# A decoder layer on one core: raw tiles of the gate block, the branch projections and the down projection laid out anew

## The chip, the cores and the metric

The kernel runs on 1 core of one Trainium2 chip. The metric is device time in microseconds, from start to end of one execution. The core's engines each run their own list of instructions in order: PE (matrix multiply, with its weight loads shown as PEld), DVE (vector), ACT (activation), POOL (GpSimd) and SP, which here issues most of the DMAs. They wait for each other by semaphores.

## What is computed

One layer of a decoder on x of 1024 positions by 1024 channels in float32. What matters for this change:

```python
g_m, g_d, g_c = jnp.split(jax.nn.sigmoid(h @ w_gate[l] + b_gate[l]), N_BRANCH, axis=-1)
merged = g_m * (y_m @ w_proj_m[l]) + g_d * (y_d @ w_proj_d[l]) + g_c * (y_c @ w_proj_c[l])
x = x + merged @ w_out[l]

h2 = rms_norm(x, norm_mlp_g[l])
x = x + jnp.square(jax.nn.relu(h2 @ w_up[l])) @ w_down[l]
```

h is the normed input; y_m, y_d and y_c are the outputs of an mLSTM, a differential attention and a cross attention, each 1024 by 1024. w_gate is 1024 by 3072, w_up 1024 by 4096, w_down 4096 by 1024.

## The kernel before

**Products in three passes.** Every float32 operand is split into two parts, hi (a cast on ACT) and lo (a subtraction on DVE): `split` (L109 to L119, its two instructions shown as L113 and L114), or `split2` (L104 to L107, shown as L106 and L69), which keeps the order of the program. `mm3` then multiplies hi by hi, hi by lo and lo by hi into one PSUM bank. So a tile that comes from memory passes SP (the load), ACT, DVE, and then PE can use it: its hi part for a product's first matmul, its lo part for the second or third.

**Winograd-like products.** The third part of the gates, the up and the down projection each form seven products of half-size blocks (`PROD`) in place of eight. The weights get four sums on POOL for this (L1161 to L1164 in the gate block, `wino_s` at L1260 to L1263 for up and down), the inputs four differences (`wino_t`, L1238 to L1246), and the seven products are recombined by seven additions on DVE into u2, c11, u3, c21.

**The order of the work around the change.** Attention (`branch_d`) runs with ordinary gate products filling PE between its steps. Its last product, po, reads two transposed tiles daT. Then come the remaining ordinary gates and the gate block (`wino_gates`, L1142): four column groups u, each with seven products of 12 matmuls, fed by raw weight tiles fr of which each group needs two; four input tiles hx (the differences of h, loaded from memory at L1189 and split) come first. A split `wsp` runs nine steps ahead of its use, and with the last split from a raw tile the next load into its ring is issued (L1176). The gate products use three PSUM banks in turn.

Then the `tail` (L1415) starts the branch projections: for each of three branches the input y comes in as eight k tiles (`k_tiles`, L1381: load kraw, split into kt), the weights in four groups of two halves (`load_w`, L132: load raw, split into w). The first group goes through the k tiles one by one (12 matmuls each, into four banks); its first half w_2207 is used with the first four k tiles, w_2209 with the others. kraw has a pool `yrp`, raw `rp2`, w `wp2`.

Last the MLP. The up projection makes 16 row tiles u; for each, `use_up` (L1516) multiplies the four recombined blocks by the norm's factor rb, applies relu and square on ACT (L1523, L1524), stores three of them, forms the four differences xts and stores these (L1528) to memory, r_d. `down` (L1565) reads them back as tiles xd (`xdma`, L1617; `xsplit`) and goes through 16 passes of four steps, each step 21 matmuls with one weight tile: wraw is loaded, summed on POOL and split into wo (`wino_steps`, L1265, whose `lead` says how many steps ahead the split runs; `side` places the work of each step). The passes 0 to 3 first load the residual x1 into their accumulators acc (L1677) on the SP queue, and an addition acc<-acc,p on DVE (or a copy on ACT) frees each PSUM bank.

Pools take their place in SBUF in the order in which they are opened, over the space of pools that are closed. With `reuse_waits="tile"` a pool waits for the old tiles under each of its tiles, one by one. Tiles are named by a counter, so numbers differ by a few between the two kernels.

Of the kernel before, what the change touches and what calls it, by code (L numbers as in the profile page):

```python
# [10 lines left out]
F32 = mybir.dt.float32  # L11
# [6 lines left out]
P = 128  # L18
# [55 lines left out]
class Layer:  # L74
# [1067 lines left out]
    def wino_gates(self, base):  # L1142
# [3 lines left out]
        tc = self.tc  # L1146
        gtp, ev, x3, x6 = one("fgt", 2), one("fev", 2), one("fx3"), one("fx6")
        x5, x4, r0, r1, r2 = one("fx5"), one("fx4"), one("fr0"), one("fr1"), one("fr2")
        rr = Ring([r2, r1, r0])
# [3 lines left out]
        raws, W = {}, []  # L1153
# [30 lines left out]
        for n in range(3):  # L1184
            load(n)
# [9 lines left out]
        tl = lambda n: ev.tile([P, 512], F32, tag=n, name=self.name(n))  # L1195
        for u in range(4):
            def out(i, c):
# [217 lines left out]
    def tail(self):  # L1415
# [11 lines left out]
        with ExitStack() as c0:  # L1427
# [68 lines left out]
            with ExitStack() as c1:  # L1496
# [19 lines left out]
                def use_up(u, cs):  # L1516

                    b = self.xrp.tile([P, 4, 512], F32, tag="xr", name=self.name("rq"))
                    V_, M = (nc.vector, G) if u == 15 else (self.V, self.V)
                    for i in (1, 3, 2, 0):  # L1520
                        hf = i % 2
                        M.tensor_mul(cs[i], cs[i], rb[:, hf * 512 : (hf + 1) * 512])
                        self.A.activation(cs[i], cs[i], AF.Relu)  # L1523
                        self.A.activation(b[:, i], cs[i], AF.Square)  # L1524
# [3 lines left out]
                    nc.sync.dma_start(self.rd[u, :, 3:7], t)  # L1528
                    yield
# [35 lines left out]
    def down(self):  # L1565
# [4 lines left out]
        with ExitStack() as c1:  # L1570
# [17 lines left out]
            wr.append(one_("dwr2"))  # L1588
            a3 = one_("acc3")
            accum(a3, 8, 768)  # L1590
            x1, x2 = one_("dx1"), one_("dx2")
            x02, wr = one_("dx02"), Ring(wr)
            wo = Ring([one_(f"dwo{i}") for i in range(3)])
            x00 = one_("dx00")
# [11 lines left out]
            raw, wsp, W = self.wino_steps([a["wdown"][g][:, kp(q)] for g, q in steps], wr, wo, 2)  # L1606
# [49 lines left out]
            n = -1  # L1656
            seen = set()
            for p, (g, qs) in enumerate(passes):
# [7 lines left out]
                for run in (qs[0:1], qs[1:2], qs[2:4]) if p == last else [(q,) for q in qs]:  # L1666
# [5 lines left out]
                    if q != qs[-1]:  # L1672
                        side(n)
# [63 lines left out]
    def run(self):  # L1737
        tc, nc = self.tc, self.nc
        with ExitStack() as ctx:
# [23 lines left out]
            with ExitStack() as c1:  # L1763
# [37 lines left out]
                with tc.tile_pool(name="wpg", bufs=13, reuse_waits="tile") as self.wp, tc.tile_pool(name="rpg", bufs=3, reuse_waits="tile") as self.rp:  # L1801
                    self.gwp, self.grp = self.wp, self.rp
                    with ExitStack() as c3:
                        E3 = lambda name, bufs: c3.enter_context(tc.tile_pool(name=name, bufs=bufs, reuse_waits="tile"))
                        pdo, pdy, pd, pd3, pdm = E3("pdo", 2), E3("pdy", 1), E3("pd", 2), E3("pd3", 3), E3("pdm", 1)
# [100 lines left out]
```

## Time and profile before

| | |
|---|---|
| runs | 2194.28, 2195.51, 2201.09 us (median 2195.51) |
| profiled execution | 2196.3 us, of which the span of the trace is 2194.5 |
| instructions | 30706, of which 11049 matmuls |
| DMA | 281.46 MB, mean 128 GB/s |

The profile is of one execution. Times in its rows are microseconds from the span's start. A wait is put down to the instruction whose end released it ("<- DVE daT L114"). The granted clock is a share of PE's full speed. Lines L are those of the kernel before; the changed kernel's stand 3 lower at the gate block and the tail (L1189 becomes L1192) and 2 to 4 lower in up and down (L1528 becomes L1530, L1617 L1619, L1677 L1681).

### The profile page before, as it was taken

What the parts mean: (1) busy time and instruction counts of PE and PEld (TensorE: products, weight loads), DVE (VectorE), ACT (ScalarE), POOL (GpSimd) and SP (SyncE); (2) the same over time, 40 slices, a digit from 0 to 9 for tenths busy, and PEclk for the clock granted to TensorE, in tenths of its full rate; (3) what the DMA queues carried; (4) which work ended last, traced back from release to release, by engine and by line L of the source; (5) the groups of instructions that cost most, each with busy time, mean ns of one, the idle gap of its engine ahead of it and who ended that gap; (6) DMA issues with size and microseconds to landing.
All of it is one profiled execution on the core that took longest, in us unless ns stands there. A gap on an engine that the chain in (4) does not pass through costs nothing.

```text
span 2194.5 us, 30706 instructions
## 1 busy us (share of the span) xinstructions
PE 2150.9 (98%) x11049; PEld 1852.4 (84%) x11049; DVE 1418.6 (65%) x2674; ACT 1002.7 (46%) x1998; POOL 565.5 (26%) x736
## 2 busy tenths in 40 slices
PE   7999999999999999999999999999999999899999
PEld 5877888898899999999888788888888788688887
DVE  6643565575548778777655433554688987767779
ACT  6543354454346666666554221223435444543332
POOL 2100000000111111111121002202756665655552
PEclk9999999999999999999999999999999999999999
DMA  6123122121443433333343643435434544844444
GB/s 246 36 73 116 59 92 68 45 81 49 161 115 92 96 97 91 84 84 83 109 148 133 207 143 127 146 111 191 154 121 173 194 155 148 328 163 158 142 142 168
DMA packets 137358, 281.46 MB, mean 128 GB/s; under 512 B 13137, under 2 KB 29814, under 8 KB 135158
## 3 DMA queue, kind: packets, MB, share of 16 engines
q1 hardware_dynamic: 130870, 259.58, 37.5%
q10 hardware_dynamic: 6336, 19.93, 2.3%
q8 instruction: 87, 1.43, 0.3%
q14 instruction: 65, 0.53, 0.1%
HBM read 182.95 MB, written 71.34 MB: 116 GB/s over the span
## 4 chain that ended last, share of the span: by engine, by line
PE 87%; DVE 5%; DMA 3%; ACT 2%; issue 1%; POOL 1%; SPq 0%; DVEq 0%; ACTq 0%; POOLq 0%
PE mm L93 51%; PE p L93 23%; PE sc L93 6%; PE po L93 3%; PE tp L96 3%; DVE acc L69 1%; DVE u L69 1%; PE pr L96 1%; DMA kraw<-y 1%; DVE wo L69 0%; DMA xd<-r_d 0%; DVE c L69 0%; PE tp L93 0%; DVE w L114 0%; DMA mx<-in_mem 0%
## 5 line engine op out<-in xcount | busy, mean ns | idle before, releaser
L93 PE MATMUL mm<-w,hT 128*128 128x384 f32 (+3 forms) x2496 | 470.6, 330 | 4.1 <-ACT w L113 3.5
L93 PE MATMUL mm<-hT,w 128*128 128x512 f32 x1680 | 413.2, 397 | 0.0
L93 PEld LDWEIGHTS mm<-w,hT 128*128 128x128 f32 x2496 | 387.7, 189 | 15.9 <-ACT w L113 4.3
L93 PEld LDWEIGHTS mm<-hT,w 128*128 128x128 f32 x1680 | 309.6, 189 | 65.1
L93 PE MATMUL p<-xd,wo 128*128 128x512 f32 x1344 | 310.5, 393 | 7.4 <-DVE xd L69 1.6
L93 PE MATMUL p<-xo,wo 128*128 128x512 f32 x1344 | 307.0, 390 | 1.2 <-DVE u L69 1.2
L93 PEld LDWEIGHTS p<-xd,wo 128*128 128x128 f32 x1344 | 253.7, 189 | 64.1 <-DVE xd L69 2.6
L93 PEld LDWEIGHTS p<-xo,wo 128*128 128x128 f32 x1344 | 251.6, 188 | 55.2 <-DVE u L69 2.8
L93 PE MATMUL mm<-kt,w 128*128 128x512 f32 x1152 | 264.1, 391 | 4.7 <-ACT kt L113 3.6
L93 PEld LDWEIGHTS mm<-kt,w 128*128 128x128 f32 x1152 | 216.9, 189 | 51.8 <-ACT kt L113 4.7
L113 ACT CAST w<-raw 128x256 fp32r<-128x256 f32 (+3 forms) x272 | 142.1, 545 | 166.6 <-PE mm L93 120.2
L106 ACT CAST wo<-wraw 128x896 fp32r<-128x896 f32 x124 | 116.8, 944 | 213.7 <-PE p L93 98.4
L114 DVE TENSOR_TENSOR w<-raw,w 128x256 fp32r<-128x256 f32 (+3 forms) x272 | 161.5, 614 | 79.9 <-ACT w L113 79.0
L69 DVE TENSOR_TENSOR wo<-wraw,wo 128x896 fp32r<-128x896 f32 x124 | 143.6, 1172 | 59.1 <-ACT wo L106 59.1
L1260 POOL TENSOR_TENSOR wraw<-wraw 128x128 f32<-128x128 f32 x128 | 93.7, 732 | 246.2 <-DMA wraw<-in_wdown 109.5
L1008 ACT ACTIVATE dpe<-sc,dst,drr 128x256 f32<-128x256 f32 (+7 forms) x128 | 106.6, 833 | 97.5 <-DVE dst L1004 95.2
L129 POOL TENSOR_SCALAR hss<-hss 128x4 f32<-128x4 f32 x8 | 3.3, 408 | 414.9 <-ACT mscr L754 273.0
L1000 DVE CUSTOM_DVE_ANT_0 sc<-sc,tmask 128x256 f32<-128x256 f32 (+7 forms) x128 | 97.0, 758 | 13.3 <-PE sc L93 12.7
L93 PE MATMUL sc<-dk,dq 128*128 128x512 f32 (+3 forms) x384 | 92.2, 348 | 0.0
L106 ACT CAST xd<-xd 128x1536 fp32r<-128x1536 f32 (+2 forms) x38 | 58.3, 1535 | 68.6 <-DMA xd<-r_d 68.6
L1263 POOL TENSOR_TENSOR wraw<-wraw 128x128 f32<-128x128 f32 x128 | 86.6, 676 | 10.0
L1262 POOL TENSOR_TENSOR wraw<-wraw 128x128 f32<-128x128 f32 x128 | 88.9, 694 | 0.0
(313 smaller groups left out, 3083.9 us busy)
## 6 DMA issues: line engine op xcount, KB each, us to landing
dk<-dsg SPq DMA_DIRECT2D x64, 256.0 KB, 4.5
wraw<-in_wup SPq DMA_DIRECT2D x64, 256.0 KB, 2.9
r_d<-xts SPq DMA_DIRECT2D x16, 1024.0 KB, 4.1
wraw<-in_wdown SPq DMA_DIRECT2D x64, 256.0 KB, 3.0
xd<-r_d SPq DMA_DIRECT2D x19, 768.0 KB, 7.3
xd<-r_d SPq DMA_DIRECT2D x14, 1024.0 KB, 6.4
raw<-in_wd SPq DMA_DIRECT2D x32, 384.0 KB, 3.3
gl<-gates SPq DMA_DIRECT2D x48, 256.0 KB, 2.7
```

The costliest lines, as they stand in the source:

```text
L69: return self.tc.keep_in_program_order(f(*a, **k))
L93: self.pin(self.nc.tensor.matmul(out, l, r, start=start, stop=stop))
L96: self.pin(self.nc.tensor.transpose(out, x, self.ident))
L106: self.A.copy(hi, src)
L113: nc.scalar.copy(hi, src)
L114: nc.vector.tensor_sub(lo, src, f32(hi))
L129: g.tensor_scalar(r, ss, 1.0 / width, EPS, op0=ALU.mult, op1=ALU.add)
L1000: V.tensor_tensor_reduce(out=sc[:, 0:n], in0=sc[:, 0:n], in1=self.tmask[:, D - n : D], scale=1.0, scalar=-3.0e38, op0=ALU.add, op1=ALU.max ...
L1008: nc.scalar.activation(pe[c][:, 0:n], sc[:, 0:n], AF.Exp, bias=t8[:, 2 + c : 3 + c], scale=rr[:, i, c : c + 1], accum_out=t8[:, 4 + c : 5 ...
L1260: G.tensor_add(r[:, 4], r[:, 0], r[:, 3])
L1262: G.tensor_sub(r[:, 6], r[:, 1], r[:, 0])
L1263: G.tensor_sub(r[:, 7], r[:, 2], r[:, 5])
```

## The change

It has three parts.

1. Gate block: two raw tiles fr in the ring in place of three, each next load two tiles ahead (`2 * u + 2 + kk`) and not three; the tiles u2, c11, u3, c21 alternate between two pools by u; the pools lie in another order, with a small unused tile between; in `branch_d` the pools pd and pd3 change places.
2. Branch projections: `yrp` has three buffers in place of two, and `yrp`, `rp2` and `wp2` wait tile by tile.
3. Up to down: the rb multiplications of u=15 go from POOL to DVE, and the differences of u=15 all to POOL (three of the four were on DVE). In down the rings of wraw and wo have four tiles in place of three, the third part of x tile 0 (`dx02`) lies elsewhere, the splits of weights run three steps ahead and not two, four weight loads and the x tiles of steps 1 to 3 are issued up front, and the side work of step 0 is placed behind the last rb multiplication.

```diff
         gtp, ev, x3, x6 = one("fgt", 2), one("fev", 2), one("fx3"), one("fx6")
-        x5, x4, r0, r1, r2 = one("fx5"), one("fx4"), one("fr0"), one("fr1"), one("fr2")
-        rr = Ring([r2, r1, r0])
+        ev1, pad, x3, x6, x4, r0, r1, x5, gtp, ev0 = (
+            one(f"f{n}", 2 if n == "gt" else 1)
+            for n in ("ev1", "pd", "x3", "x6", "x4", "r0", "r1", "x5", "gt", "ev0")
+        )
+        rr, ev = Ring([r1, r0]), (ev0, ev1)
...
                 if j == 6:
-                    load(2 * u + 3 + kk)
+                    load(2 * u + 2 + kk)
...
-                    rawp = E(name="yrp", bufs=2)
-                    self.rp = E(name="rp2", bufs=2)
-                    self.wp = E(name="wp2", bufs=4)
+                    rawp = E(name="yrp", bufs=3, reuse_waits="tile")
+                    self.rp = E(name="rp2", bufs=2, reuse_waits="tile")
+                    self.wp = E(name="wp2", bufs=4, reuse_waits="tile")
...
-                    V_, M = (nc.vector, G) if u == 15 else (self.V, self.V)
                     for i in (1, 3, 2, 0):
-                        M.tensor_mul(cs[i], cs[i], rb[:, hf * 512 : (hf + 1) * 512])
+                        self.after = self.V.tensor_mul(cs[i], cs[i], rb[:, hf * 512 : (hf + 1) * 512])
...
-                    t = self.wino_t(b, V_)
+                    t = self.wino_t(b, G if u == 15 else self.V)
...
-            raw, wsp, W = self.wino_steps([a["wdown"][g][:, kp(q)] for g, q in steps], wr, wo, 2)
+            raw, wsp, W = self.wino_steps([a["wdown"][g][:, kp(q)] for g, q in steps], wr, wo, 3)
...
             xdma(0)
-            raw()
-            raw()
+            for _ in range(4):
+                raw()
+            xdma(1)
+            xdma(2)
+            xdma(3)
+            xsplit(2)
             xsplit(0, split=self.split)
-            wsp(0, self.split, False)
-            xdma(1)
+            wsp(0, self.split)
             xsplit(1, split=self.split)
-            wsp(0)
-            xdma(2)
-            xsplit(2, (0,))
-            wsp(0)
-            xsplit(2, (1, 2))
-            xdma(3)
+            wsp(0, self.split)
+            wsp(0, self.split)
...
-                    if q != qs[-1]:
+                    if n == 0:
+                        with tc.issue_after(self.after.ins):
+                            side(n)
+                    elif q != qs[-1]:
                         side(n)
```

How the order of instructions moves is shown at three places. At the entry to the gate block, DVE's list before; daT is the pair of attention tiles, hx the gate block's inputs, fr and raw are raw weights and w their split tiles:

```order
L1060 SCALAR_TENSOR_TENSOR doS_2009_11897<-po_2037_12046,dst_2006_11868,doS_2009_11897 128x128
L114 TENSOR_TENSOR w_2069_12344<-fr_2066_12303,w_2069_12344 128x256
L114 TENSOR_TENSOR w_2070_12347<-fr_2067_12310,w_2070_12347 128x256
L114 TENSOR_TENSOR w_2071_12350<-fr_2066_12303,w_2071_12350 128x256
L114 TENSOR_TENSOR w_2072_12353<-fr_2067_12310,w_2072_12353 128x256
L114 TENSOR_TENSOR w_2073_12356<-fr_2066_12303,w_2073_12356 128x256
L114 TENSOR_TENSOR daT_2047_12109<-tp_2046_12104,daT_2047_12109 128x512
L114 TENSOR_TENSOR hx_2062_12299<-hx_2062_12299 128x2x512 x2
L114 TENSOR_TENSOR daT_2049_12126<-tp_2048_12121,daT_2049_12126 128x512
L1060 SCALAR_TENSOR_TENSOR doS_2009_11897<-po_2050_12129,dst_2021_11951,doS_2009_11897 128x128
```

And after:

```order
L1060 SCALAR_TENSOR_TENSOR doS_2009_11897<-po_2037_12046,dst_2006_11868,doS_2009_11897 128x128
L114 TENSOR_TENSOR w_2068_12342<-fr_2066_12308,w_2068_12342 128x256
L114 TENSOR_TENSOR hx_2063_12305<-hx_2063_12305 128x2x512 x2
L114 TENSOR_TENSOR daT_2047_12109<-tp_2046_12104,daT_2047_12109 128x512
L114 TENSOR_TENSOR daT_2049_12126<-tp_2048_12121,daT_2049_12126 128x512
L1060 SCALAR_TENSOR_TENSOR doS_2009_11897<-po_2050_12129,dst_2021_11951,doS_2009_11897 128x128
```

Four gate weight splits are gone from here to a later place, and the splits of an hx tile have moved from between the two daT tiles to ahead of both.

At the end of the gate block and the start of the branch projections, DVE's list before; mm is a PSUM bank, u and c the recombined gates, raw a half of the projection's weights and kraw a tile of y:

```order
L1222 TENSOR_TENSOR c21_2176_12899<-u3_2175_12898,mm_2184_12955 128x512
L114 TENSOR_TENSOR w_2207_13170<-raw_2206_13168,w_2207_13170 128x1024
L1225 TENSOR_TENSOR u3_2175_12898<-u3_2175_12898,mm_2186_12972 128x512
L1226 TENSOR_TENSOR u2_2173_12896<-u2_2173_12896,mm_2186_12972 128x512
L114 TENSOR_TENSOR w_2209_13175<-raw_2208_13173,w_2209_13175 128x1024
L1229 TENSOR_TENSOR u2_2173_12896<-u2_2173_12896,mm_2188_12990 128x512
L1446 MEMSET hole_13071 128x1
L114 TENSOR_TENSOR kt_2191_13130<-kraw_2190_13128,kt_2191_13130 128x1024
L114 TENSOR_TENSOR kt_2193_13135<-kraw_2192_13133,kt_2193_13135 128x1024
L114 TENSOR_TENSOR w_2223_13296<-raw_2222_13294,w_2223_13296 128x1024
```

And after:

```order
L114 TENSOR_TENSOR kt_2191_13136<-kraw_2190_13134,kt_2191_13136 128x1024
L1225 TENSOR_TENSOR c21_2176_12904<-u3_2175_12903,mm_2184_12960 128x512
L114 TENSOR_TENSOR kt_2193_13141<-kraw_2192_13139,kt_2193_13141 128x1024
L114 TENSOR_TENSOR kt_2195_13146<-kraw_2194_13144,kt_2195_13146 128x1024
L1228 TENSOR_TENSOR u3_2175_12903<-u3_2175_12903,mm_2186_12977 128x512
L1229 TENSOR_TENSOR u2_2173_12901<-u2_2173_12901,mm_2186_12977 128x512
L114 TENSOR_TENSOR kt_2197_13151<-kraw_2196_13149,kt_2197_13151 128x1024
L1232 TENSOR_TENSOR u2_2173_12901<-u2_2173_12901,mm_2188_12995 128x512
L1449 MEMSET hole_13077 128x1
L114 TENSOR_TENSOR kt_2199_13156<-kraw_2198_13154,kt_2199_13156 128x1024
L114 TENSOR_TENSOR kt_2201_13161<-kraw_2200_13159,kt_2201_13161 128x1024
L114 TENSOR_TENSOR w_2207_13176<-raw_2206_13174,w_2207_13176 128x1024
```

The first k tiles now stand among the last gate additions, and the first weight half w_2207 has moved from ahead of all k tiles to behind six of them.

From up to down, the SP queue before; xts is the stored tile of differences (xts_2839 of u=14, xts_2845 of u=15), xd an x tile read back, acc an accumulator:

```order
L1617 DMA xd_2858_18294<-r_d 128x3x512
L1617 DMA xd_2859_18296<-r_d 128x4x512
L1274 DMA wraw_2861_18303<-in_wdown 128x512
L1617 DMA xd_2862_18311<-r_d 128x3x512
L1617 DMA xd_2863_18313<-r_d 128x4x512
L1274 DMA wraw_2871_18343<-in_wdown 128x512
L1617 DMA xd_2872_18349<-r_d 128x3x512
L1617 DMA xd_2873_18351<-r_d 128x2x512
L1617 DMA xd_2874_18353<-r_d 128x2x512
L1528 DMA r_d<-xts_2845_18146 128x2048
L1274 DMA wraw_2876_18381<-in_wdown 128x512
L1274 DMA wraw_2878_18413<-in_wdown 128x512
```

And after, the same stretch of SP's queue:

```order
L1619 DMA xd_2856_18295<-r_d 128x3x512
L1619 DMA xd_2857_18297<-r_d 128x4x512
L1619 DMA xd_2858_18299<-r_d 128x3x512
L1619 DMA xd_2859_18301<-r_d 128x4x512
L1277 DMA wraw_2861_18316<-in_wdown 128x512
L1277 DMA wraw_2863_18329<-in_wdown 128x512
L1277 DMA wraw_2865_18338<-in_wdown 128x512
L1619 DMA xd_2875_18381<-r_d 128x3x512
L1619 DMA xd_2876_18383<-r_d 128x2x512
L1530 DMA r_d<-xts_2845_18152 128x2048
L1277 DMA wraw_2874_18375<-in_wdown 128x512
L1619 DMA xd_2877_18385<-r_d 128x2x512
```

The x tiles of three steps and three weight tiles now come in one row; the store of u=15 is still ahead of the accumulator loads, which follow a few entries further on in both. On POOL before, the multiplications of u=15:

```order
L1263 TENSOR_TENSOR wraw_2857_18288<-wraw_2857_18288 128x128
L1522 TENSOR_TENSOR c11_2841_18121<-c11_2841_18121,rb2_13027 128x512
L1522 TENSOR_TENSOR c21_2843_18123<-c21_2843_18123,rb2_13027 128x512
L1522 TENSOR_TENSOR u3_2842_18122<-u3_2842_18122,rb2_13027 128x512
L1260 TENSOR_TENSOR wraw_2861_18303<-wraw_2861_18303 128x128
L1262 TENSOR_TENSOR wraw_2861_18303<-wraw_2861_18303 128x128
L1261 TENSOR_TENSOR wraw_2861_18303<-wraw_2861_18303 128x128
L1263 TENSOR_TENSOR wraw_2861_18303<-wraw_2861_18303 128x128
L1522 TENSOR_TENSOR u2_2840_18120<-u2_2840_18120,rb2_13027 128x512
L1243 TENSOR_TENSOR xts_2845_18146<-rq_2844_18132 128x512
```

And on POOL after, the differences of u=15:

```order
L1266 TENSOR_TENSOR wraw_2863_18329<-wraw_2863_18329 128x128
L1263 TENSOR_TENSOR wraw_2865_18338<-wraw_2865_18338 128x128
L1245 TENSOR_TENSOR xts_2845_18152<-rq_2844_18138 128x512
L1246 TENSOR_TENSOR xts_2845_18152<-rq_2844_18138 128x512
L1247 TENSOR_TENSOR xts_2845_18152<-rq_2844_18138,xts_2845_18152 128x512
L1264 TENSOR_TENSOR wraw_2865_18338<-wraw_2865_18338 128x128
L1248 TENSOR_TENSOR xts_2845_18152<-rq_2844_18138,xts_2845_18152 128x512
L1265 TENSOR_TENSOR wraw_2865_18338<-wraw_2865_18338 128x128
```

The four multiplications have left POOL, and all four differences stand on it.

More of the change, by code (lines that the diff above doesn't have):

```diff
@@ L1146, in wino_gates @@
         tc = self.tc
-        gtp, ev, x3, x6 = one("fgt", 2), one("fev", 2), one("fx3"), one("fx6")
-        x5, x4, r0, r1, r2 = one("fx5"), one("fx4"), one("fr0"), one("fr1"), one("fr2")
-        rr = Ring([r2, r1, r0])
+        ev1, pad, x3, x6, x4, r0, r1, x5, gtp, ev0 = (
+            one(f"f{n}", 2 if n == "gt" else 1)
+            for n in ("ev1", "pd", "x3", "x6", "x4", "r0", "r1", "x5", "gt", "ev0")
+        )
+        nc.vector.memset(pad.tile([P, 32], F32, tag="pad", name="fpd")[:, 0:1], 0.0)
+        rr, ev = Ring([r1, r0]), (ev0, ev1)
         X = {}
@@ L1182, in x_ @@
             return self.hT[:, 2 * kp + k, i, hf * 512 : hf * 512 + 512]
-        for n in range(3):
+        for n in range(2):
             load(n)
@@ L1194, in wino_gates @@
         self.pinned = True
-        tl = lambda n: ev.tile([P, 512], F32, tag=n, name=self.name(n))
         for u in range(4):
+            tl = lambda n: ev[u % 2].tile([P, 512], F32, tag=n, name=self.name(n))
             def out(i, c):
@@ L1587, in down @@
             accum(a2, 4, 0)
-            wr.append(one_("dwr2"))
+            wo = [one_("dwo0")]
             a3 = one_("acc3")
-            accum(a3, 8, 768)
+            accum(a3, 8, 0)
             x1, x2 = one_("dx1"), one_("dx2")
-            x02, wr = one_("dx02"), Ring(wr)
-            wo = Ring([one_(f"dwo{i}") for i in range(3)])
-            x00 = one_("dx00")
+            wr = Ring(wr + [one_("dwr2"), one_("dwr3")])
+            wo = Ring(wo + [one_(f"dwo{i}") for i in (1, 2, 3)])
+            x00, x02 = one_("dx00"), one_("dx02")
             accs = accs[2:] + accs[:2]
@@ L1804, in run @@
                         E3 = lambda name, bufs: c3.enter_context(tc.tile_pool(name=name, bufs=bufs, reuse_waits="tile"))
[L1805 removed]
+                        pdo, pdy, pd3, pd, pdm = E3("pdo", 2), E3("pdy", 1), E3("pd3", 3), E3("pd", 2), E3("pdm", 1)
                         pdv2, pds, pd5, pdv = E3("pdv2", 17), E3("pds", 1), E3("pd5", 7), E3("pdv", 5)
```

## The prediction

> **What bounds the kernel now.** The page of the profile comes first, then busy time by stretch, for the whole span and for the three places that the diff touches.
>
> ```profile
> PE 2150.9 (98%) x11049; PEld 1852.4 (84%) x11049; DVE 1418.6 (65%) x2674; ACT 1002.7 (46%) x1998; POOL 565.5 (26%) x736
> ```
>
> PE is busy for 98% of the span, and the change takes no matmul away. So only PE's gaps and PE's slow stretches can be gained. Columns below: the stretch and its length, busy time (instructions) of PE, PEld, DVE, ACT and POOL, granted clock, DMA share, GB/s.
>
> ```profile
> 1100.00:1131.00 31.00, 29.41 (x139) 24.54 (x138) 18.61 (x25) 18.02 (x29) 4.81 (x7) 0.94 0.45 161
> 1202.00:1240.00 38.00, 33.31 (x136) 25.79 (x135) 20.39 (x21) 16.53 (x18) 0.20 (x1) 0.96 0.71 244
> 1872.00:1898.00 26.00, 18.64 (x71) 13.10 (x69) 22.02 (x18) 15.79 (x18) 21.21 (x17) 0.95 0.79 297
> 1898.00:1910.00 12.00, 11.94 (x42) 9.10 (x42) 7.60 (x10) 6.68 (x9) 5.28 (x12) 0.81 0.93 336
> 1910.00:2160.00 250.00, 250.00 (x1105) 207.07 (x1104) 183.62 (x188) 95.30 (x90) 141.87 (x212) 1.00 0.50 164
> ```
>
> Most of the down projection has no gap: 250 us for 1105 matmuls, 0.226 us each, so 12 of them (one gate product, or one k tile) take 2.72 us. PE is idle for 1.6 us at the entry to the gate block (1100 to 1131), 4.7 at the start of the branch projections (1202 to 1240) and 7.4 between up and down (1872 to 1898). Behind each of these the granted clock falls:
>
> ```profile
> 1107.00:1110.00 3.00, 3.00 (x12) 2.52 (x11) 1.04 (x2) 1.00 (x2) 0.00 (x0) 0.52 0.56 184
> 1110.00:1113.00 3.00, 3.00 (x14) 2.47 (x13) 0.69 (x1) 0.69 (x1) 1.21 (x2) 0.91 0.92 322
> 1215.00:1218.00 3.00, 2.23 (x6) 1.77 (x7) 2.25 (x2) 1.76 (x2) 0.00 (x0) 0.73 0.88 328
> 1218.00:1221.00 3.00, 3.00 (x11) 2.37 (x10) 0.20 (x1) 0.00 (x0) 0.00 (x0) 0.70 0.86 250
> 1896.00:1899.00 3.00, 3.00 (x7) 1.94 (x8) 3.00 (x2) 2.81 (x4) 0.15 (x1) 0.50 0.98 270
> 1899.00:1902.00 3.00, 3.00 (x9) 2.35 (x8) 0.30 (x1) 2.84 (x4) 1.54 (x4) 0.50 1.03 388
> ```
>
> Lost to the clock, as length times (1 - clock): 1.4 + 0.3 = 1.7 us at the gate entry, 0.8 + 0.9 = 1.7 at the branch projections, 3.0 at down. With the idle time the three places hold 3.3 + 6.4 + 10.4 = 20.1 us, 0.9% of the span. That is all that these edits can win.
>
> **1. Gate entry and gate block.** PE's one wait at the entry (us in total, times, longest), and what stood on DVE ahead of the tile that it waited for (start, duration):
>
> ```profile
> PE po L93 <- DVE daT L114: 1.6, 1, 1.6
> ...
> 1103.12 2.78 DVE L114 TENSOR_TENSOR hx<-hx 128x1024 fp32r<-128x1024 f32 x2 [0.26 <-ACT hx L113]
> 1105.82 0.68 DVE L114 TENSOR_TENSOR daT<-tp,daT 128x512 fp32r<-128x512 f32 x1
> ```
>
> Before, the two splits of an hx tile (2.78 us) stand between daT_2047 and daT_2049, and PE's last attention product needs both. After, an hx tile's splits stand ahead of both daT tiles, whose splits follow each other. SP's load of that hx waits for ACT's last activation of the scores and so is issued about when it was, 1094.5, but without four fr loads right ahead of it. (A DMA row ends with KB each and the median us to landing.)
>
> ```profile
> 1094.56 0.37 SPq L1189 DMA_DIRECT2D hx<-hc_d  x1
> hx<-hc_d SPq DMA_DIRECT2D x1, 1024.0 KB, 5.9
> 1102.02 2.02 ACT L113 CAST hx<-hx 128x1024 fp32r<-128x1024 f32 x2
> 1103.60 1.36 PE L93 MATMUL po<-dv,daT 128*128 128x256 f32 x9
> ```
>
> At 5.9 us hx lands at 1100.4; with half of the bytes gone I estimate 4.5, 1099, and take 1099.8. ACT's first cast (1.0) ends at 1100.8, DVE's two splits (1.39 each) at 1103.6, daT_2047 at 1104.3, daT_2049 at 1105.0, where it was 1106.5 before. PE, ready at 1103.6, waits 0.7 us instead of 1.6, and I take it that so short a wait leaves the clock alone: 0.9 + 1.7 = 2.6 gained. If hx lands later than by the 5.9 row, or the clock falls all the same, nothing is gained; if it lands at 1099, 3.2. So 0 to 3.2. The fr tile that now loads at about 1105 is covered by 84 matmuls (19 us) of the ordinary gates.
>
> Inside the block two raw tiles take the place of three. At each new u the first split from a new raw tile stands ahead of the c11 addition, which frees a PSUM bank. In before one such place shows:
>
> ```profile
> PE mm L93 <- DVE c L1215: 0.2, 1, 0.2
> fr<-in_wgq SPq DMA_DIRECT2D x9, 256.0 KB, 4.2
> ```
>
> A load is issued at the same split as before, but is now wanted at all three later u. I take 0.2 more twice: 0.4 us lost, between 0 and 2 (4.7 for 4.2 to landing at each u, with the clock not halved).
>
> **2. Start of the branch projections.** PE's longest wait before, and the DMA and engine rows that price the new order:
>
> ```profile
> PE mm L93 <- ACT kt L113: 3.6, 2, 3.0
> ...
> 1206.49 1.22 DVE L114 TENSOR_TENSOR kt<-kraw,kt 128x1024 fp32r<-128x1024 f32 x1
> 1214.67 1.04 ACT L113 CAST kt<-kraw 128x1024 fp32r<-128x1024 f32 x1 [1.45 <-DMA kraw<-y]
> kraw<-y SPq DMA_DIRECT2D x4, 512.0 KB, 5.8
> raw<-in_wpc SPq DMA_DIRECT2D x2, 512.0 KB, 4.3
> ```
>
> Before, weights come first on DVE and each k tile is late. After, the loads start sooner, because the pools wait by tile: three kraw tiles once the third of the seven products of the gates' last u is done, four products (4 x 2.72 = 10.9 us) before the gates' end, which I call G. But six k tiles are now split ahead of w_2207, the weights that the first matmul needs, and only four of those tiles are used with it. In order: first landings at about G-6.5; kt_2191, 2193, 2195 split by G-1.2, and each frees the raw tile for one of the next three, so kraw_2200 is issued at G-1.2. At about 4 us to landing (4.3 is the nearest row with little else in flight) it is there at G+3; its cast (1.04) and that of w_2207 end at G+5, DVE's splits of the two (1.22 each) at G+6.4. PE's first matmul needs the cast, its third the split: idle 5.0 + 0.9 = 6 us, and 1.7 for the clock, 7.7 in all against 6.4. After that all tiles are ahead of PE. So 1.3 us lost. With 3.3 to landing it would be 0.7 gained; with 5.8, the row of the crowded stretch, every link moves: kraw_2200 is issued at G+0.7, lands at G+6.5, w_2207 is split at G+9.9, and with the clock the gap is 11.3 to 13, some 6 lost.
>
> **3. From up to down.** What PE waited for, and the chain that held the accumulators, before (SP, DVE, POOL; start, duration):
>
> ```profile
> PE p L93 <- DVE xd L69: 1.6, 1, 1.6
> PE p L93 <- DVE wo L69: 1.6, 1, 1.6
> PE p L93 <- ACT wo L106: 1.6, 1, 1.6
> ...
> 1894.64 0.33 SPq L1528 DMA_DIRECT2D r_d<-xts  x1
> 1896.47 2.62 SPq L1677 DMA_DIRECT2D acc<-x_d  x4
> 1903.70 0.84 DVE L69 TENSOR_TENSOR acc<-acc,acc 128x512 f32<-128x512 f32 x1 [4.40 <-DMA acc<-x_d]
> 1904.47 2.46 DVE L69 TENSOR_TENSOR acc<-acc,p 128x512 f32<-128x512 f32 x4
> 1889.46 1.77 POOL L1243 TENSOR_TENSOR xts<-rq 128x512 f32<-128x512 f32 x1 [1.41 <-ACT rq L1524]
> ```
>
> SP stands at the store of u=15 until its transform is done (1894.64); the accumulator loads are behind it, and pass 1's third product needs the bank that the first acc,p addition frees, at about 1905.2: 10.55 us after the store. After, the x and weight loads of four steps are issued early, so PE's first four steps should run with some 3 us of waits, to about 1896. But the store stays ahead of the accumulators in SP's queue, so what counts is when POOL has finished its four subtractions (three of them DVE's before).
>
> ```profile
> 1856.05 1.28 DVE L69 TENSOR_TENSOR c<-c,rb 128x512 f32<-128x512 f32 x2
> xd<-r_d SPq DMA_DIRECT2D x3, 768.0 KB, 10.1
> 1878.58 1.46 ACT L106 CAST xd<-xd 128x1536 fp32r<-128x1536 f32 x1
> 1879.95 0.63 ACT L1524 ACTIVATE rq<-c 128x512 f32<-128x512 f32 x1
> ```
>
> DVE has its seven additions of u=15 (0.62 each, by the acc row's shape), a split and the multiplications (0.64) done by about 1881, which is before ACT comes to them: on ACT the cast of xd_2858 is now ahead of the activations. Its load waits for the step before up's last (1872 less 21 matmuls, 1867.3) and lands between 1877.4 (10.1 us) and 1880.4 (some 6 MB queued since 1865, at the rows' best rate of 388 GB/s). The cast (1.46) ends at 1879 to 1881.8, the eight activations (0.57 to 0.63) at 1884.0 to 1886.5; middle 1885.2. POOL then takes 4 x 1.77 and one weight sum (0.54 to 1.17, rows below): 1893.1, only 1.5 us sooner. The third product starts at 1903.7, after 7 us of idle PE, which costs 1.7 of clock once it resumes. Together 0.2 us lost; between 4 gained (POOL done at 1891, clock kept) and 3 lost (1894.8, and 3.0 of clock). What would have made the early loads pay is spent in this one wait.
>
> **A rule on the clock.** In the rows one wait of 1.6 us at the gate entry is followed by 3 us at 0.52. The Trainium skill, TensorE: Matmul & The Clock Gate, "Part 1: The HAM clock gate", says that the array drops to half rate after at least one idle window of about 3.4 us in a free-running count, and comes back after as long busy. The trace agrees with the length of the slow stretch and not with the trigger, 1.6 being less than a window; by the page alone the slow 3 us had another cause than this wait and would stay, and the sum be 1.7 worse, which the gate term's range holds already.
>
> **Sum.** -2.6 + 0.4 + 1.3 + 0.2 = -0.7 us on the profiled run's 2196.3 (span 2194.5, and 1.8 around it): 2195.6. That run is 0.8 over the median of the three, so 2194.8 on the median's scale.
>
> **Rivals.**
> *Faster:* the early loads land as in the light rows. Gate entry -3.0, nothing lost inside the block, branch projections -0.7, down -4: 7.7 gained, 2187.8 on the median's scale. For it: the loads stand where nothing holds them. Against it: DMA at a share of 0.93 to 1.05 around 1900.
> *All three gaps close:* at most 20 us, 2175.4. It needs POOL's transform and the accumulators to be hidden, which SP's order speaks against.
> *k tiles late:* 5.8 us to landing, 6 lost there, -2.6 + 0.4 + 6 + 0.2 = +4.0: 2199.5. No gain, but within 0.3%.
> *POOL late, slower than before:* the four subtractions run beside DVE's splits of xd, two operands from SBUF each. POOL's weight sums show what that costs, 1171 ns against 537 in the long part of down:
>
> ```profile
> L1261 POOL TENSOR_TENSOR wraw<-wraw 128x128 f32<-128x128 f32 x3 | 3.5, 1171 | 0.0
> L1261 POOL TENSOR_TENSOR wraw<-wraw 128x128 f32<-128x128 f32 x53 | 28.5, 537 | 0.0
> ```
>
> At 2.18 times 1.77 a subtraction takes 3.86, POOL ends at 1885.2 + 15.4 + 1.2 = 1901.8, the third product starts at 1912.4, and with 1.7 of clock 8.9 are lost: +8.0, 2203.5. It turns the whole slower once POOL ends after about 1894, and slower by over 0.3% after about 1900.5. Against it: the xts row at 1889.46 took 1.77 while DVE subtracted too. The Trainium skill, SBUF — State Buffer, "Who interferes with whom", states that a DVE instruction with two SBUF inputs contends with a GpSimd one that reads SBUF and that the later blocks fully; the weight sums agree, the xts row does not.
> *That the change does nothing* can't be: the order of instructions moves at all three places.
>
> **How the numbers follow.** 0.3% is 6.6 us, about what a measurement of this kernel can tell from no change. Forecast 0.45, faster rival 0.25, all gaps 0.05, k tiles late 0.12, POOL late 0.13. Faster by over 0.3%: 0.25 + 0.05 + 0.03 from the forecast's good end = 0.33. Slower by over 0.3%: 0.13 + 0.02 of the k tiles' bad end = 0.15. Within: 0.52. The range leaves out all gaps and POOL late, 0.18: from 2185 (the faster rival with the inside of the block and the clock at their good ends) to 2201 (k tiles late at 13 us). The forecast's own range, with the bounds of its terms: 2190 to 2199.
>
> **What would show it.** Right: a wait of po on daT of under 1 us, and a clock near 1.00 at 1107; a first matmul on kt that waits 4 to 6 us for w; PE idle for 5 us or more in pass 1 of down until DVE's acc addition, with the store of u=15 issued at 1892 to 1895. Wrong: an accumulator load before about 1892, w_2207 split before kt_2199, or c11 holding PE at each u for more than 1 us.

## The result and the profile after

| | before | after |
|---|---|---|
| median of 5 runs | 2196.97 us (2194.28 to 2201.09) | 2210.25 us (2209.13 to 2212.3) |
| profiled execution, its span | 2196.3, 2194.5 | 2209.13, 2207.4 |

The changed kernel is slower: ratio 1.0062, 95% interval 1.005 to 1.0075, some 13.6 us. The forecast was 2194.8 (2185 to 2201), so both the number and the range were wrong. Four executions among the experiments that took over 3000 us (one of run 7, its profiled one, and three of the kernel before) are left out of the ratios.

PE's row of the page of after, and then stretches of after at the three places, with the last two rows cut finer (columns: the stretch and its length, busy time and instructions of PE, PEld, DVE, ACT and POOL, granted clock, DMA share, GB/s).

```profile
PE 2153.9 (98%) x11049; PEld 1853.6 (84%) x11049; DVE 1419.3 (64%) x2676; ACT 1000.7 (45%) x1998; POOL 570.8 (26%) x735
```

```profile
1090.00:1131.00 41.00, 40.65 (x204) 33.86 (x203) 25.26 (x40) 24.38 (x43) 5.59 (x6) 1.00 0.53 184
1202.00:1240.00 38.00, 32.00 (x128) 25.41 (x127) 20.35 (x22) 13.98 (x15) 0.20 (x1) 0.87 0.74 249
1872.00:1898.00 26.00, 21.27 (x85) 15.48 (x84) 21.96 (x20) 16.94 (x19) 12.91 (x11) 0.98 0.68 267
1898.00:1920.00 22.00, 9.58 (x29) 7.29 (x29) 6.56 (x9) 6.11 (x7) 11.73 (x19) 0.66 0.70 252
...
1212.00:1218.00 6.00, 5.79 (x14) 4.22 (x14) 3.76 (x4) 4.08 (x5) 0.00 (x0) 0.51 0.94 357
1916.00:1920.00 4.00, 4.00 (x10) 3.17 (x11) 4.00 (x6) 0.00 (x0) 0.00 (x0) 0.50 0.77 283
```

The stretch from 1898 to 1920 in the kernel before:

```profile
1898.00:1920.00 22.00, 21.94 (x86) 17.39 (x86) 13.99 (x16) 11.43 (x13) 12.66 (x22) 0.90 0.94 339
```

Most of the loss stands in one row: from 1898 to 1920 PE is busy for 9.58 of 22 us, before for 21.94, and the clock is halved when it resumes. The gap of before was in the row from 1872 to 1898; the early loads filled part of that one (PE idle for 4.7 us in place of 7.4) and a longer one opened behind it. The entry to the gate block is clean (40.65 of 41, clock 1.00).

The starts of PE's products show where the 12.9 us by which the spans differ arise. PE is 0.6 us sooner than before when it comes to the gate entry, a difference that arises in the first 100 us, which the change doesn't touch. It gains 2.9 at the entry, loses 3.5 inside the block, 2.8 from there to the end of up (1.8 of it in the first 35 us, at the projections, and 1.0 by one more wait in up, near 1724), and 10.1 from the end of up to the end of the span.

**Up to down.** PE's rows from the end of up (start, duration, in brackets the idle time ahead and what ended it):

```profile
1874.74 1.52 PE L93 MATMUL p<-xd,wo 128*128 128x512 f32 x6
...
1894.84 0.49 PE L93 MATMUL p<-xd,wo 128*128 128x512 f32 x1 [1.46 <-ACT xd L106]
1897.16 6.39 PE L93 MATMUL p<-xd,wo 128*128 128x512 f32 x20 [1.83 <-DVE xd L69]
1915.98 14.21 PE L93 MATMUL p<-xd,wo 128*128 128x512 f32 x51 [12.42 <-DVE acc L69]
```

Followed back: the bank is freed by DVE's acc addition, that waits for an accumulator's load, the load stands behind the store of u=15 in SP's queue, and the store waits for POOL. DVE, SP and ACT first, then POOL's list from up's end:

```profile
1914.63 0.69 DVE L69 TENSOR_TENSOR acc<-acc,acc 128x512 f32<-128x512 f32 x1 [15.44 <-DMA acc<-x_d]
```

```profile
1903.28 0.33 SPq L1530 DMA_DIRECT2D r_d<-xts  x1
...
1906.95 7.92 SPq L1681 DMA_DIRECT2D acc<-x_d  x12
```

```profile
1886.29 1.14 ACT L1526 ACTIVATE rq<-u 128x512 f32<-128x512 f32 x2
```

```profile
1885.04 1.31 POOL L1263 TENSOR_TENSOR wraw<-wraw 128x128 f32<-128x128 f32 x1 [12.94 <-DMA wraw<-in_wdown]
1886.31 2.50 POOL L1265 TENSOR_TENSOR wraw<-wraw 128x128 f32<-128x128 f32 x1
...
1891.97 0.46 POOL L1263 TENSOR_TENSOR wraw<-wraw 128x128 f32<-128x128 f32 x1
...
1894.50 0.45 POOL L1263 TENSOR_TENSOR wraw<-wraw 128x128 f32<-128x128 f32 x1
1894.91 3.34 POOL L1245 TENSOR_TENSOR xts<-rq 128x512 f32<-128x512 f32 x1
1898.21 2.12 POOL L1246 TENSOR_TENSOR xts<-rq 128x512 f32<-128x512 f32 x1
...
1901.96 1.29 POOL L1248 TENSOR_TENSOR xts<-rq,xts 128x512 f32<-128x512 f32 x1
```

ACT has rq ready at 1887.4. POOL idles 12.94 us for the load of a weight tile, then sums two whole weight tiles and one sum of a third, and comes to the first difference at 1894.91, 7.5 us after its input was there. The loads of these weights stand behind the x tiles that are now issued early; KB each and median us to landing of what was issued from 1872 to 1892:

```profile
xd<-r_d SPq DMA_DIRECT2D x1, 1024.0 KB, 13.5
wraw<-in_wdown SPq DMA_DIRECT2D x3, 256.0 KB, 10.8
```

**Gate block and branch projections.** Waits of PEld in the block, before and then after (us in total, times, longest; c is c11, the u of L1223 is u3):

```profile
PEld mm L93 <- DVE c L1215: 0.6, 1, 0.6
```

```profile
PEld mm L93 <- DVE c L1218: 2.0, 3, 0.8
PEld mm L93 <- DVE u L1223: 1.8, 3, 0.7
```

Waits of PE after, over both places:

```profile
PE mm L93 <- issue: 5.8, 1, 5.8
...
PE po L93 <- DVE daT L114: 0.2, 1, 0.2
```

PE's first hx product and the start of its last product of the block, before and then after:

```profile
1134.05 11.04 PE L93 MATMUL mm<-hx,w 128*128 128x512 f32 x48
...
1202.61 2.88 PE L93 MATMUL mm<-hT,w 128*128 128x512 f32 x12
```

```profile
1130.52 2.96 PE L93 MATMUL mm<-hx,w 128*128 128x512 f32 x12
...
1202.54 2.90 PE L93 MATMUL mm<-hT,w 128*128 128x512 f32 x12
```

Two rows of ACT after, which casts the weights that stand ahead of c11 and of u3 on DVE, and then PE and ACT after at the start of the projections:

```profile
1132.10 0.41 ACT L113 CAST w<-fr 128x256 fp32r<-128x256 f32 x1 [3.51 <-DMA fr<-in_wgq]
...
1138.02 1.02 ACT L113 CAST w<-fr 128x256 fp32r<-128x256 f32 x3 [2.06 <-POOL fr L1165]
```

```profile
1211.23 1.19 PE L93 MATMUL mm<-kt,w 128*128 128x512 f32 x2 [5.79 <-issue]
```

```profile
1210.09 1.04 ACT L113 CAST w<-raw 128x1024 fp32r<-128x1024 f32 x1
```

The block's first hx product starts at 1130.52, 3.5 us sooner than before (1134.05); 0.6 of this stood already ahead of the entry. But its last product starts at 1202.54, before at 1202.61: all that was won is lost inside, where the first raw tile of each new u holds c11 and then u3 three times (3.8 us of weight loads that wait, before 0.6). At the projections PE is idle for 6.0 us; its wait is put down to "issue", but ends with ACT's cast of the first weights (1211.13). Up ends at 1874.74, 2.8 later than before.

### The profile page after: what moved, and what is told of

It is laid out like the page before. It is cut to its first block, busy times and chain, and to the rows that moved or that the text cites. A ratio compares the mean times of both kernels' runs of the same rounds, so it can differ in the third digit from the quotient of the medians.

```text
span 2207.4 us, 30706 instructions
## 1 busy us (share of the span) xinstructions
PE 2153.9 (98%) x11049; PEld 1853.6 (84%) x11049; DVE 1419.3 (64%) x2676; ACT 1000.7 (45%) x1998; POOL 570.8 (26%) x735
## 4 chain that ended last, share of the span: by engine, by line
PE 87%; DVE 4%; DMA 4%; POOL 2%; ACT 2%; issue 1%; SPq 0%; DVEq 0%; POOLq 0%; ACTq 0%
PE mm L93 50%; PE p L93 24%; PE sc L93 6%; PE po L93 3%; PE tp L96 3%; DMA fr<-in_wgq 1%; PE pr L96 1%; DMA wraw<-in_wdown 1%; DVE w L114 0%; PE tp L93 0%; DVE acc L69 0%; DVE u L69 0%; DMA mx<-in_mem 0%; DVE xts L69 0%; DMA raw<-in_wkv 0%
## 5 line engine op out<-in xcount | busy, mean ns | idle before, releaser
L93 PE MATMUL p<-xd,wo 128*128 128x512 f32 x1344 | 311.0, 393 | 17.2 <-DVE acc L69 12.4
```

Of the source, the lines that this page charges most:

```text
L93: self.pin(self.nc.tensor.matmul(out, l, r, start=start, stop=stop))
```

## The experiments

Theory: POOL's list between up and down holds the store of u=15, and with it the accumulators. Rivals: the gate block and the projections cost as much; DMA is simply full; the loss inside the gate block comes of its two raw tiles. Ratios are to the kernel before, with the 95% interval; times are medians. Differences "by the ratios" are between two versions' ratios.

**1. All but the down projection.** Parts 1 and 2 of the change, with part 3 left out.

> Gate block and branch projections as changed, up and down as before. Theory (the loss is in the turn from up to down): the gain at the gate entry and the losses inside the block and at the branch projections leave +1 to +3 us over the kernel before, 2198 to 2200; PE's longest wait around 1900 falls from 12.4 us to under 2. Rival (the new layout of the gate block and of the projections costs something later too): it stays within 4 us of the changed kernel, 2206 or more.

2199.0 us, ratio 1.0012 (1.0002 to 1.0022). So some 11 of the 13.6 us belong to part 3, and 2.6 to the first two. The traces agree: from down's first product to the end of the span it is 322.5 us before, 332.7 in the changed kernel and 322.6 here.

**2. The differences of u=15 back on DVE**, but for the one that `wino_t` always gives POOL.

```diff
-                    t = self.wino_t(b, G if u == 15 else self.V)
+                    t = self.wino_t(b, self.V)
```

> The changed kernel, with three of the four differences of u=15 back on DVE and one on POOL. Theory (POOL's list holds the store of u=15, and the store holds the accumulators): POOL's one difference still stands behind its weight sums until about 1895, but the store is issued at about 1897 and not 1903.3; PE's wait falls from 12.4 to about 6 us, and the time to about 2204. Rival (the DMAs are full anyway, and the accumulators land when they land): the wait falls by less than 2 us.

2206.08 us, ratio 1.0045 (1.003 to 1.006): 3.7 us less by the ratios, whose intervals overlap; in the traces down is 3.3 us shorter. PE's wait of 12.4 us fell to 5.1, more than the rival allows, but a new one of 4.9 stands ahead of it, for an x tile's split on DVE. The store was expected at 1897 and was issued at 1902.16, 26.3 us behind up's end (28.5 in the changed kernel), for this reason (POOL, then SP):

```profile
1886.78 2.09 POOL L1263 TENSOR_TENSOR wraw<-wraw 128x128 f32<-128x128 f32 x1 [13.78 <-DMA wraw<-in_wdown]
...
1897.53 2.50 POOL L1263 TENSOR_TENSOR wraw<-wraw 128x128 f32<-128x128 f32 x1
1900.00 2.13 POOL L1246 TENSOR_TENSOR xts<-rq 128x512 f32<-128x512 f32 x1
```

```profile
1902.16 0.33 SPq L1530 DMA_DIRECT2D r_d<-xts  x1
```

One difference behind the weight sums holds the store nearly as four do. The nine sums ahead of it take 13.2 us here and 9.9 in the changed kernel; the longest, of 1.97 to 2.50, run beside DVE's splits of x tiles, which come later here. So the place in the list costs more than the number of differences.

**3. The accumulator loads of pass 0 ahead of the store.** They are issued before the first pass and left out of it.

```diff
+            for j, f, hf in ((1, 0, 1), (6, 0, 0), (4, 1, 1), (5, 1, 0)):
+                nc.sync.dma_start(acc[0][j], half(self.x1d, f, hf))
             n = -1
             seen = set()
```

> The changed kernel, with the four accumulator loads of pass 0 issued on SP ahead of the store of u=15. Theory: POOL is as late as before (store at 1902 to 1904), but PE's wait of 12.4 us falls to under 3, and the clock behind it stays up: 10 to 12 us less, about 2199. Rival (the DMAs are full from the early x tiles): the accumulators land after 1908 all the same, or push the x tiles back, and the time falls by less than 4 us.

2200.71 us, ratio 1.0021 (1.0011 to 1.003): 9 us less by the ratios. The store is no sooner (1906.79; up ended 3 us later in this profile), yet PE's longest wait there is 1.8 us. So the store's part was to hold the loads behind it, and a DMA that is simply full falls as a cause: the four loads are now in the same crowded stretch as the x and weight tiles. SP and PE:

```profile
1881.11 6.83 SPq L1658 DMA_DIRECT2D acc<-x_d  x4
...
1906.79 0.32 SPq L1530 DMA_DIRECT2D r_d<-xts  x1
```

```profile
1909.10 14.12 PE L93 MATMUL p<-xd,wo 128*128 128x512 f32 x61 [1.75 <-ACT acc L1689]
```

**4. The first weight halves of the projections behind four k tiles**, not six.

```diff
-                        ys = self.k_tiles(ysp, rawp, self.yd[b])
+                        ys = self.k_tiles(ysp, rawp, self.yd[b], range(4) if bi == 0 else range(NK))
+                        if bi == 0:
+                            w0 = self.load_w(a["wpc"][0], 256, 4)
+                            with ExitStack() as behind:
+                                for i in self.first:
+                                    behind.enter_context(tc.issue_after(i.ins))
+                                ys += self.k_tiles(ysp, rawp, self.yd[b], range(4, NK))
```

> The changed kernel, with the branch projections' first two weight halves split behind four k tiles and not behind six and eight. If the first matmul waits for w_2207 behind k tiles that it doesn't need: PE starts on kt at about 1209 and not at 1211.2, 2 to 3 us less with the clock, 2207 to 2208. If what holds it is the memory under w_2207 (the gates' last tiles) or the loads: no change.

2206.89 us, ratio 1.0048 (1.0033 to 1.0063), 3.1 us less by the ratios, whose intervals overlap. The wait ahead of the projections' first product falls from 5.8 to 3.6 us.

**5. The weight sums behind the four differences.** As in the changed kernel, but the sums of three weight tiles are placed after the last difference.

```diff
+            def wraw_behind():
+                wsp(0, self.split, False)
+                with tc.issue_after(self.sub.ins):
+                    raw()
...
-            wsp(0, self.split)
+            wraw_behind()
```

> The changed kernel, with POOL's sums of the weight tiles 2861, 2863 and 2865 put behind the four differences of u=15; nothing else moves on SP ahead of the store. If POOL is late because two weight tiles stand ahead of the differences (7.5 us of the 8.5 by which the store is late): the store goes from 28.5 us after the end of up to about 21, PE's wait of 12.4 us falls to about 5, and some 7 us are won, 2202 to 2204. If POOL is late because its subtractions themselves are slow beside DVE (8.4 us for the four where 7.1 was reckoned): the store moves by less than 2 us. If the cover is thin: the weight casts behind those sums hold the x tile of step 3 on ACT, and 3 us or more of wait appear there.

2201.57 us, ratio 1.0031 (1.0018 to 1.0045): 6.8 us less by the ratios, with as many instructions on each compute engine as in the changed kernel. POOL, SP and DVE:

```profile
1886.15 1.74 POOL L1245 TENSOR_TENSOR xts<-rq 128x512 f32<-128x512 f32 x1 [15.54 <-ACT rq L1526]
...
1892.82 1.27 POOL L1248 TENSOR_TENSOR xts<-rq,xts 128x512 f32<-128x512 f32 x1
```

```profile
1894.12 0.33 SPq L1530 DMA_DIRECT2D r_d<-xts  x1
```

```profile
1897.15 1.18 DVE L69 TENSOR_TENSOR wo<-wraw,wo 128x896 fp32r<-128x896 f32 x1 [5.55 <-ACT wo L106]
1898.25 2.54 DVE L69 TENSOR_TENSOR xd<-xd 128x2048 fp32r<-128x2048 f32 x1
```

POOL now waits for rq, not for a load, and the store is 20.9 us behind up's end (1873.25), where the prediction had put it at 21. The theory holds. What is late next is the split of an x tile on DVE, which ends at 1900.79 and for which PE waits 7.5 us. The tile itself is there (ACT has cast it by 1887.9), but its split stands behind that of a weight tile, which waits for ACT's cast and so for the sums that now come later on POOL. The third of the expectations, a thin cover, came true on DVE and not on ACT.

**6. As 5, with the accumulator loads of 3, and the split of the second part of step 3's x tile ahead of that of the weight tile that waits for POOL.**

> As the run before, with the accumulator loads of pass 0 also ahead of the store, and the split of step 3's x tile ahead of the weight split that waits for POOL. Theory: nothing of what POOL does late is then on PE's path except the banks that ACT copies out behind one weight cast (2 to 4 us): 2198 to 2201. If the DMAs are the bound of this stretch: not below the run with the early accumulators alone, 2200.7.

2197.55 us, ratio 1.0011 (1.0002 to 1.002). No wait of PE over 1.7 us is left from up to down, but the short ones still add up to 7.1 us, before to 7.4. So the long wait is gone, the mended down takes 320.9 us to the end of the span where that of before takes 322.5, and the whole is still no faster than before.

**7. Three raw tiles in the gate block**, as before, without the small unused tile; the order of the other pools is that of the change.

```diff
-        for n in range(2):
+        for n in range(3):
...
-                    load(2 * u + 2 + kk)
+                    load(2 * u + 3 + kk)
...
-        rr, ev = Ring([r1, r0]), (ev0, ev1)
+        rr, ev = Ring([r1, r0, r2]), (ev0, ev1)
```

> The changed kernel, with three raw tiles in the gate block's ring again (each next load three ahead; the order at the entry stays as changed). If the 3.4 us that the gate entry wins are lost inside the block because each u waits for its first raw tile and for POOL's sums of it: the weight loads' waits at c and u3 in the block (3.8 us in all) fall to under 1, and 2 to 3.5 us are won in the block, 2207 to 2208 in all. If the block's loss is due to the new places in memory: no change.

2211.54 us, ratio 1.0076 (1.0061 to 1.0091): a miss, nothing gained, as the rival "new places in memory" had it. The trace of run 8, with the same gate block, shows where the time goes.

**8. The edits of 4, 6 and 7 together.**

> The second run of this call with three raw tiles in the gate block and the projections' first weight halves behind four k tiles. If the single effects add (-10 to -12, -3.4, -2 to -3): 2192 to 2196, faster than both kernels or equal to the one before. If they hide each other in DMA: 2197 or more.

2195.73 us, ratio 1.0003 (0.9994 to 1.0012): no difference from before that can be told. In its gate block the waits for c11 shrink from 2.0 to 0.3 us, but there is one new wait (PE, then ACT and DVE):

```profile
1140.98 4.48 PE L93 MATMUL mm<-hx,w 128*128 128x512 f32 x12 [2.35 <-DVE u L1223]
```

```profile
1135.86 2.00 ACT L113 CAST hx<-hx 128x1024 fp32r<-128x1024 f32 x2 [1.78 <-DMA hx<-hc_d]
```

```profile
1136.94 3.29 DVE L113 TENSOR_TENSOR hx<-hx 128x1024 fp32r<-128x1024 f32 x2 [1.47 <-ACT hx L113]
1140.16 0.68 DVE L1223 TENSOR_TENSOR u<-u,mm 128x512 f32<-128x512 f32 x1
```

With three raw tiles and no pad the last hx tile is loaded later (1128.22 on SP, in the changed kernel by 1106.8); its split (3.29 us) now stands inside the block, ahead of the u3 addition that frees a bank. That the two raw tiles are the cause of the loss in the block is neither borne out nor excluded: undoing them moved the loss.

**9. The gate block alone** (part 1 only).

> Only the gate block and the pool order of the branch stage are those of the changed kernel; the branch projections' pools, up and down are those of before. Theory (the 3.5 us won at the gate entry are lost again inside the block, where the gate products' last stretch starts at the same time in both traces): the time is that of before, 2195.5 to 2196.7, and the waits of the weight loads for DVE's c and u are there as in the changed kernel, 3 to 4 us in all. Rival (the block gained 2.6 us as predicted, and the projections cost more than they show): 2193 to 2194.

2202.16 us, ratio 1.0028 (1.0017 to 1.0039): 6.1 us slower, and both theories had said faster or no change. The block itself ends as before, but the projections behind it don't start:

```profile
1214.26 30.94 PE L93 MATMUL mm<-kt,w 128*128 128x512 f32 x124 [9.18 <-DMA kraw<-y]
```

```profile
1208.55 1.04 ACT L113 CAST kt<-kraw 128x1024 fp32r<-128x1024 f32 x1 [2.78 <-DMA gates<-gt]
...
1213.11 1.04 ACT L113 CAST w<-raw 128x1024 fp32r<-128x1024 f32 x1 [2.89 <-DMA gates<-gt]
```

The k tiles come first here too, as in the changed kernel, so this order comes with the gate block's layout. And ACT waits twice, 5.7 us, for the store of a gate; in the changed kernel's rows ACT has no such wait. That the pools of the next stage lie under the gates' tiles is inferred from this releaser, not shown otherwise. The first weights are cast at 1213.11, and PE starts right behind, whatever its wait is put down to.

**10. The branch projections alone** (part 2 only).

> Only the three raw tiles and the tile by tile waits of the branch projections are those of the changed kernel. Theory: all of the 2.9 us that the run without the new down cost is here, so 2198 to 2199.5, with one wait of TensorE ahead of the first key product of 5 to 6 us. Rival (the projections gain by the earlier loads and the gate block loses): 2194 to 2196.

2195.27 us, ratio 0.9999 (0.999 to 1.0008): no change, within the rival's range and not what the theory expected. (In its trace PE gains 1.7 us between 1203 and 1240, which the interval neither shows nor excludes.) The weights are still cast ahead of the k tiles, as before (ACT):

```profile
1202.28 1.05 ACT L113 CAST w<-raw 128x1024 fp32r<-128x1024 f32 x1 [7.98 <-DMA raw<-in_wpc]
...
1205.84 1.03 ACT L113 CAST kt<-kraw 128x1024 fp32r<-128x1024 f32 x1
```

**11. The mended down alone** (the down of run 6; gate and projections of before).

> Gate and projections of before; the down projection of the changed kernel with the weight sums behind POOL's differences, the accumulator loads early and the x halves ahead of the third weight. Theory (parts add): the run with all of the change and these three edits took 2197.55, gate and projections are worth +2.95 of it, so 2194.6 (2193.5 to 2195.7), a little faster than before. Rival (the new down is no better than the old one even so): 2196 to 2197.

2195.13 us, ratio 0.9992 (0.9983 to 1.0002). At best a little faster than before; the interval still contains 1.

**12. All of the change with the edits of 6 and 4**, two raw tiles as changed.

> All of the change, with the three edits of the down projection and the first weight halves of the projections behind four k tiles; two raw tiles in the gate block as changed. Theory (a third raw tile in the gate block gains nothing or costs 1.6 us, and the weight's place gives 3.4 us): 2194.1 (2193.2 to 2195.2). Rival (the third raw tile was worth something in the run with all edits): 2196 to 2197.5.

2194.95 us, ratio 0.9999 (0.9989 to 1.0008). The weights' place gave 2.6 us beside run 6 (by the ratios, whose intervals overlap). Against run 8 the third raw tile makes no difference that these intervals tell. No version beats the kernel before measurably.

## Why the prediction was wrong

**The step that failed** is in part 3: "POOL then takes 4 x 1.77 and one weight sum". The inputs were ready when the prediction said (12.7 us after up's end, reckoned 13.2) and the four differences cost nearly what it said (8.0 us for 7.1). But POOL runs nine weight sums ahead of the first difference, two whole tiles and one sum of a third, as its rows above show. The first of them can't start before its load lands (10.8 us, behind the early x tiles), and they run beside DVE's splits. This moved the store from 21 us behind up's end to 28.5. Run 5 undoes just this and lands on the 20.9. From the store to the third product the prediction had 10.55 us, the trace 12.7, and once PE resumes the clock costs 2.5 us (half rate from 1916 to 1920, 0.87 in the 4 us behind) where 1.7 was reckoned. So of this part, reckoned +0.2, between -4 and +3, the terms now add up to 0.2 + 7.4 + 2.2 + 0.8 = 10.6; the runs say about 11 (run 1 against all).

**The rival** "POOL late" had the right place, the right sign and the tipping point (POOL done after about 1900.5; it was 1903.3, or 1900.5 if the 2.8 us by which up ends later are taken off), with 0.13 as its chance. Its own mechanism, differences of 3.86 each, was not the one: they took 1.28 to 3.34. That its time came near is in part luck. A slow POOL was weighed, a POOL that waits for a load was not, though the order ahead of the prediction shows the weight loads behind the x tiles and weight sums right ahead of the differences.

**Gate entry:** right. Predicted 2.6 gained (0 to 3.2), measured 2.9; the wait fell from 1.6 to 0.2 us and the clock stayed at 1.00. The Trainium skill, TensorE: Matmul & The Clock Gate, "Part 1: The HAM clock gate", lets the clock fall after an idle window of about 3.4 us, by which shortening this wait would have changed nothing in the clock. The traces decide: the three in which PE waits 1.6 to 1.7 us here (before, runs 10 and 11) have a half-rate stretch of 3.413 us right behind it, and the ten in which it waits 0.54 us or less (after, runs 1 to 6, 8, 9 and 12) have none there.

**Inside the block:** the mechanism was right (the first raw tile's split ahead of c11 at each u), the size not: 0.4 predicted, about 3.4 measured, beyond its bound of 2. A second addition, u3, was held as well, by the sums on POOL: the weight split ahead of it waits for a cast, and that for the sums (the row at 1138.02).

**Branch projections:** the sum was near (1.3 lost predicted, 1.8 by PE's place at 1240; idle 6.0 us as reckoned, and 2.9 lost to the clock from 1212 to 1218 in place of 1.7), its cause only half right. The order, the first weights behind six k tiles, held. But the prediction had the loads start sooner "because the pools wait by tile", and runs 9 and 10 say otherwise. With the tile waits alone the first load of a k tile is issued at 1200.9, as before (1200.1), the weights stay first and the time is that of before. With the gate block's new layout alone it is issued at 1193.2, as in the changed kernel (1194.3), the k tiles come first and 6.1 us are lost; together it is 2.6 (run 1). So it is part 1 that costs, and part 2 gives some 3.5 of it back. Against the runs with one part each, the gate's terms (-2.6 and +0.4) were off by 8.3 us and the projections' by 1.5; together, -0.9 against 2.6, by 3.5.

**What stays open:** whether the block can keep what the entry wins; it loses over 3 us with either number of raw tiles, by different waits. A layout that keeps the last hx tile ahead of the block and three raw tiles wasn't tried.

## What to carry to other kernels

When loads are issued earlier, read the in-order list of every engine that consumes them and ask what stands behind the first consumer: here a short transform on the path stood behind work that waited for an early load, and moving it ahead of that work gave 6.8 us with the same number of instructions on each compute engine. Then ask what stands behind the work that was moved: here it was another split that PE needed. A store in a queue of loads holds all of them until its data is ready; put loads that don't need that data ahead of it. And price edits of the memory layout together with the stage that comes next, since a pool's place can decide when the next stage's loads start: two parts gave 6.1 and -0.2 us singly and 2.6 together.

## What the runs showed of the hardware

- POOL's weight sums of 128x128 took 0.45 to 0.47 us wherever DVE was idle beside them (109 of the 512 in the trace of after), and 0.45 to 0.48 where DVE read one of its inputs from PSUM (139). Beside DVE's splits and other operations with both inputs in SBUF, 108 of 120 took over 0.6 and up to 2.51; the other 144 had a mix beside them. The Trainium skill, SBUF — State Buffer, "Who interferes with whom", says that the two engines contend when a DVE instruction has two inputs from SBUF; the rows agree in kind.
- A 256 KB load took 10.8 us to land behind the x tiles of 768 and 1024 KB (the median of three), against a median of 3.1 over all 64 loads of the down weights in the same profile.
- In the record of the granted clock that the traces keep, the half-rate stretches inside the span last 3.41 us or two, three or four times as long (in after 3.413, 10.24 and 13.653; in before 3.413 and 6.827), but for the one at its very end. So slow stretches come in steps, and what PE loses in one depends on how busy it is there.
